# Begin addresses of weight-part and activation buffers moved by multiples of 32 and 16 bytes in a two-layer fp32 encoder

## The chip, the core and the metric

The kernel runs on one core of one Trainium2 chip. The metric is the device time of one execution, in microseconds: 2274.97 us for the kernel before, the median of 3 runs (2274.55 to 2275.17).

## What is computed

An encoder trunk of two layers over 256 tokens of width 2048, in fp32. Layer 0 is neighbourhood attention (16 heads of 128, a learned position bias) and a squared-ReLU MLP of hidden width 8192; layer 1 is a dilated attention of three groups with partial rotary, merged by softmax weights, and a second MLP of the same size:

```python
for i in range(DEPTH):
    hn = rms_norm(x, mixer_norms[i])
    x = x + (neighbourhood_attention if i == 0 else dilated_attention)(hn, ...)
    x = x + jnp.square(jax.nn.relu(rms_norm(x, g) @ w1)) @ w2
return rms_norm(x, final_norm)
```

Nearly all the work is products of a 256-row activation with weight matrices that are read once from memory, some 426 MB of them.

## The kernel before

**Numbers in two parts.** A weight or an activation v in fp32 is split into hi, which is v rounded to the format float32r, and lo, which is v minus hi, rounded in the same way. A product is then hi·hi + hi·lo + lo·hi, three matmuls into the same accumulator (`three`, L193; its lines are L195, L196, L197). ScalarE (ACT) makes hi by a copy (L190), VectorE (DVE) makes lo by a subtraction (L191); both lines are in `split`.

**Steps.** The program is a list of 400 steps. A step holds four 128x512 blocks of weights, loaded by SyncE into a buffer `w` (three of these), and split into parts two blocks at a time: `two_parts` (L138) takes a buffer `wh` and a buffer `wl` of 1024 elements a partition from a pool with four buffers of each. The matmuls of a step come in four quarters; between the quarters stand the splits for the step two ahead, and attention's small work.

**Who streams.** In the query and key products of attention (`gemm_cols`, L200) the weights are the stationary operand and the activation streams: L220 streams hi and lo of the activation side by side (512 columns) past wh, L222 streams hi alone (256 columns) past wl. Everywhere else (`gemm_rows`, `gemm_pair`) a 128x128 piece of the activation is stationary and 512 columns of wh or wl stream past it. Every matmul is preceded by its own weight load (PEld), which lies beside the matmul ahead of it.

**Activations.** They lie in buffers of 2048 elements a partition: four of `xT` (the normalized input of a layer, transposed) and four of the tag `o`, which serve as `oT` (attention's output), `hT` (the MLP's hidden values) and, at times, as score and bias buffers.

**The x-steps.** In the MLP some pairs of blocks are multiplied by a scheme that takes seven products where eight would be needed. For these the step forms sums of weight blocks (`sums`, with the parts `hs` and `ls`), and sums of activation blocks (`xs` in the first product of an MLP; in the second a smaller tile that is also named `hs`). These parts lie in the stage's own pool, outside the pools that the change touches. Seven products of three matmuls take the forms (xs with hs), (xs with wh), (xT with hs) and (xT with wh), so the same matmul form appears with operands from different pools.

**Order.** The order of instructions on each engine is written out by hand; no scheduler decides it.

**Where the buffers begin.** In the program as built, the pools are laid one behind the other in each partition. `xT`'s four buffers begin at the bytes 33952, 42144, 50336, 58528; the four of `o` at 66720 and on by 8192; `w`'s three at 99488 and on by 8192; `wh`'s at 124064 and on by 4096; `wl`'s at 140448 and on by 4096. All of these leave the remainder 32 when divided by 128. The tiles of a stage's own pool (`xs`, `sums`, `hs`, `ls`, `C`, the attention tiles) begin at 159616 and behind; all that enter float32r matmuls leave the remainder 0, as does the identity matrix `ident`.

Of the kernel before, what the change touches and what calls it, by code (L numbers as in the profile page):

```python
# [9 lines left out]
F32R = mybir.dt.float32r  # L10
# [4 lines left out]
P = 128  # L15
T = 256
# [31 lines left out]
def tile_encoder(ctx: ExitStack, tc: tile.TileContext, ins, out):  # L48
# [3 lines left out]
    xpool = ctx.enter_context(tc.tile_pool(name="xpool", bufs=4))  # L52
    opool = ctx.enter_context(tc.tile_pool(name="opool", bufs=4))
    wpool = ctx.enter_context(tc.tile_pool(name="wpool", bufs=3))
    hlpool = ctx.enter_context(tc.tile_pool(name="hlpool", bufs=4))
# [15 lines left out]
    class Part:  # L71

        pool = guard = None
# [15 lines left out]
    def scratch(shape, name):  # L89

        if part.name[0] == "f":
            return part.pool.tile(shape, F32, name=name, tag="t", bufs=2)
        return part.pool.tile(shape, F32, name=name, tag="p", bufs=5)
# [41 lines left out]
    def add(engine, out, a, b):  # L135
        engine.tensor_tensor(out=out, in0=a, in1=b, op=ALU.add)  # L136

    def two_parts(s, u):  # L138
        hi = hlpool.tile([P, 2, 512], F32R, name="wh", tag="wh")
        lo = hlpool.tile([P, 2, 512], F32R, name="wl", tag="wl")  # L140
        for a in range(2):
            s.hi[2 * u + a], s.lo[2 * u + a] = hi[:, a, :], lo[:, a, :]
        return hi, lo
# [45 lines left out]
    def split(dst_hi, dst_lo, src):  # L189
        nc.scalar.copy(dst_hi, src)  # L190
        nc.vector.tensor_tensor(out=dst_lo, in0=src, in1=dst_hi.bitcast(F32), op=ALU.subtract)  # L191
# [159 lines left out]
    def last_sum(q, tb, c, out):  # L351

        C, own = q["C"][:, 2 * tb + c, :], q[STD[tb, c]]
        if (tb, c) == (1, 0):
            subtract(nc.vector, out, own, C)
        else:
            add(nc.vector, out, C, own)


    class Norm:  # L360
# [18 lines left out]

        def parts(self, c, half):  # L380
            if half == 0:
                self.xT[c] = xpool.tile([P, 4, 2, T], F32R, name="xT", tag="xT")
            xT = self.xT[c]
            if 2 * c + half in self.pairs:
                raw = scratch([P, 2, T], "gx")
                for a in range(2):
                    k = 4 * c + 2 * half + a
                    nc.scalar.activation(raw[:, a, :], self.tp[:, a, :], AF.Copy, scale=gT[:, self.n, k:k + 1])
                self.sums[2 * c + half] = part.pool.tile([P, 2, 3, P], F32R, name="xs", tag="xs", bufs=len(self.pairs))
                sums_and_parts(raw, xT, half, self.sums[2 * c + half])  # L390
                return
            for which, a in [(which, 2 * half + a) for which in ("hi", "lo") for a in range(2)]:
                src = self.tp[:, a % 2, :]
                hi, lo = xT[:, a, 0, :], xT[:, a, 1, :]
                if self.perm:
                    src = src.rearrange("p (j s r) -> p r s j", s=4, r=4)
                    hi = hi.rearrange("p (r s j) -> p r s j", s=4, r=4)
                    lo = lo.rearrange("p (r s j) -> p r s j", s=4, r=4)
                g = gT[:, self.n, 4 * c + a:4 * c + a + 1]
                if which == "hi":  # L400
                    nc.scalar.activation(hi, src, AF.Copy, scale=g)
                elif self.perm:
                    gx = scratch([P, T], "gx")
                    nc.vector.tensor_scalar(out=gx.rearrange("p (r s j) -> p r s j", s=4, r=4), in0=src,
                                            scalar1=g, scalar2=None, op0=ALU.mult)
                    nc.vector.tensor_tensor(out=xT[:, a, 1, :], in0=gx, in1=xT[:, a, 0, :].bitcast(F32),
                                            op=ALU.subtract)
                else:
                    nc.vector.scalar_tensor_tensor(out=lo, in0=src, scalar=g, in1=hi.bitcast(F32),
                                                   op0=ALU.mult, op1=ALU.subtract)  # L410
# [31 lines left out]
    def sums_and_parts(raw, t, half, sums):  # L442

        c = scratch([P, 3, P], "c")
        a11, a21, a12, a22 = raw[:, 0, :P], raw[:, 0, P:], raw[:, 1, :P], raw[:, 1, P:]
        subtract(nc.vector, c[:, 0, :], a11, a21)
        subtract(nc.vector, a21, a21, a22)
        subtract(nc.vector, c[:, 1, :], a11, a21)
        subtract(nc.vector, c[:, 2, :], a12, c[:, 1, :])
        hi, lo = (t[:, 2 * half:2 * half + 2, h, :] for h in range(2))  # L450
        nc.scalar.copy(hi, raw)
        nc.scalar.copy(sums[:, 0], c)
        subtract(nc.vector, lo, raw, hi.bitcast(F32))
        subtract(nc.vector, sums[:, 1], c, sums[:, 0].bitcast(F32))
# [36 lines left out]
    def at(i, pe=None, post=None, quarter=1):  # L491
        later.append((i, pe, post, quarter))
# [3 lines left out]
    def at_after(i, n, f):  # L496
        later_after.append((i, n, f))
# [20 lines left out]
    na_oT = [None] * 4  # L518
# [12 lines left out]
    class NaHeads:  # L531
# [73 lines left out]

        def s3_post(self, h):
            if na_oT[self.c] is None:
                na_oT[self.c] = opool.tile([P, 4, 2, T], F32R, name="oT", tag="o")
            t = na_oT[self.c]
            split(t[:, h, 0, :], t[:, h, 1, :], self.o[:, 0, :])  # L610

# [16 lines left out]
    for c in range(4):  # L628
# [5 lines left out]
        i = steps.index(made[0])  # L634
# [5 lines left out]
        i = steps.index(made[0])  # L640
# [26 lines left out]
    def ffn(norm, w1, w2, next_norm, next_done):  # L667
        for g in range(4):
            last = g == 3
            pairs2 = (3, 5) if last else (2, 3, 5)  # L670
            hT, sums = [None] * 4, {}

            def hidden(made, q, cp, hT=hT, sums=sums, pairs2=pairs2, last=last):
                i = steps.index(made[-1]) + 1

                def squared_relu(tb, n):
                    c = q["C"][:, 2 * tb + n, :]
                    nc.scalar.activation(c, c, AF.Relu, scale=norm.r[:, tb:tb + 1])  # L678
                    nc.scalar.activation(c, c, AF.Square)

                for m, (tb, n) in enumerate(QUARTERS):
                    made[-1].after[m].append(lambda tb=tb, n=n: last_sum(q, tb, n, q["C"][:, 2 * tb + n, :]))
                    at_after(i, m, lambda tb=tb, n=n: squared_relu(tb, n))
                for r in range(4):
                    held = {}

                    def pe(r=r, held=held):
                        held["t"] = t = ps.misc()
                        for a in range(2):
                            f = 2 * r + a  # L690
                            for tb in range(2):
                                nc.tensor.transpose(t[:, a, tb * P:(tb + 1) * P],  # L692
                                                    q["C"][:, 2 * tb + f // 4, f % 4 * P:(f % 4 + 1) * P], ident)

                    def post(r=r, held=held):
                        c, half, pair = 2 * cp + r // 2, r % 2, 4 * cp + r
                        if half == 0:
                            hT[c] = opool.tile([P, 4, 2, T], F32R, name="hT", tag="o")
                        if pair in pairs2:
                            raw = part.pool.tile([P, 2, T], F32, name="h", tag="h", bufs=2)  # L700
                            nc.scalar.copy(raw, held["t"])

                            def parts_of(c=c, half=half, raw=raw, pair=pair):
                                sums[pair] = part.pool.tile([P, 2, 3, P], F32R, name="hs", tag="hsum", bufs=3)
                                sums_and_parts(raw, hT[c], half, sums[pair])
                            steps[i + (3 if cp else 2 * r - 1)].after[1].append(parts_of)
                        else:
                            to = hT[c][:, 2 * half:2 * half + 2]
                            split(to[:, :, 0, :], to[:, :, 1, :], held["t"])

                    at(i + 1, pe, post, quarter=r)
# [66 lines left out]
    dil_oT = [None] * 2  # L778
# [21 lines left out]
    class DilHeads:  # L800
# [91 lines left out]

        def s3_post(self, h):
            if dil_oT[self.hh] is None:
                dil_oT[self.hh] = opool.tile([P, 4, 2, T], F32R, name="oT", tag="o")
            t = dil_oT[self.hh]
            src = self.o[:, 0, :].rearrange("p (r s j) -> p j s r", r=4, s=4)
            hi = t[:, h, 0, :].rearrange("p (j s r) -> p j s r", r=4, s=4)
            lo = t[:, h, 1, :].rearrange("p (j s r) -> p j s r", r=4, s=4)
            nc.scalar.copy(hi, src)  # L900
            nc.vector.tensor_tensor(out=lo, in0=src, in1=hi.bitcast(F32), op=ALU.subtract)
# [132 lines left out]
    for i, s in enumerate(steps):  # L1034
# [31 lines left out]
        if i:  # L1066
            p = steps[i - 1]
# [67 lines left out]
```

## Time and profile before

| what | value |
|---|---|
| median of 3 runs | 2274.97 us |
| profiled execution, from its first to its last instruction | 2273.7 us |
| its mean granted TensorE clock | 0.999 |
| matmuls, busy | 2252.3 us, 10,904 of them |
| DVE busy | 1876.6 us |
| ACT busy | 1263.4 us |
| read from memory | 426.38 MB |

The profiled execution lies 1.3 us below the median of the runs. In the profile "PE" is the matmul and "PEld" the weight load. A matmul's duration reaches from its start to the modelled end of its last column, so that it overlaps the next one: the pace is read from the starts in the timeline, and the duration tells how one matmul differs from another of the same form. A view by tile gives the least, the median and the greatest duration of every form that reads or writes a tile.

### The profile page before, as it was taken

Reading aid. Unit: us, or ns where it says so; the run is one execution under the profiler, and the core shown is the slowest. Engines: PE = TensorE matmul, PEld = TensorE weight load, DVE = VectorE, ACT = ScalarE, POOL = GpSimd, SP = SyncE. Lnnn points to the kernel's source line nnn. Section 1 sums busy time; section 2 is a strip of 40 time slices with the busy share of each in tenths; the row PEclk is TensorE's granted clock in tenths of the full one; section 3 lists DMA queues with packets and bytes.
Section 4 is the critical chain, followed back from the end, with each engine's and each line's share of the span. In section 5 each row is a group of like instructions: output and inputs, shape, how many; then the busy total and the mean of one; then the engine's idle time right before and its main releaser. Section 6 shows DMA issues by size and latency. Waiting matters only on the chain.

```text
span 2273.7 us, 28396 instructions
## 1 busy us (share of the span) xinstructions
PE 2252.3 (99%) x10904; PEld 1882.5 (83%) x10904; DVE 1876.6 (83%) x2215; ACT 1263.4 (56%) x1570; POOL 0.7 (0%) x6
## 2 busy tenths in 40 slices
PE   9999999999999999999999999999999999999998
PEld 7888888888888888888888888888888888888886
DVE  6777666899999999989877667757999999999988
ACT  6545445665565565565444544456665665665664
POOL 0000000000000000000000000000000000000000
PEclk9999999999999999999999999999999999999999
DMA  7556655556656666655555545454666666666664
GB/s 252 185 178 187 185 181 167 185 185 208 199 185 205 203 185 195 205 179 190 206 177 183 178 167 185 167 173 149 209 199 196 190 198 193 198 195 196 202 213 138
DMA packets 110728, 430.33 MB, mean 189 GB/s; under 512 B 23872, under 2 KB 24448, under 8 KB 92160
## 3 DMA queue, kind: packets, MB, share of 16 engines
q1 hardware_dynamic: 109920, 426.82, 58.5%
q8 instruction: 85, 1.39, 0.2%
q10 hardware_dynamic: 672, 1.70, 0.2%
q14 instruction: 51, 0.42, 0.1%
HBM read 426.38 MB, written 2.10 MB: 188 GB/s over the span
## 4 chain that ended last, share of the span: by engine, by line
PE 92%; DVE 4%; ACT 2%; issue 1%; DMA 0%; SPq 0%; ACTq 0%; DVEq 0%
PE banks L195 23%; PE banks L197 23%; PE banks L196 23%; PE banks L220 13%; PE banks L222 7%; DVE wl L191 1%; PE banks L692 1%; DVE C L136 1%; DVE sums L136 1%; ACT wh L190 0%; PE banks L378 0%; ACT hs L176 0%; ACT C L678 0%; DVE C L133 0%; PE banks L890 0%
## 5 line engine op out<-in xcount | busy, mean ns | idle before, releaser
L191 DVE TENSOR_TENSOR wl<-w,wh 128x1024 fp32r<-128x1024 f32 (+1 forms) x802 | 966.0, 1218 | 297.0 <-ACT wh L190 293.3
L190 ACT CAST wh<-w 128x1024 fp32r<-128x1024 f32 (+1 forms) x802 | 829.6, 1048 | 589.3 <-PE banks L197 324.1
L220 PE MATMUL banks<-xT,wh 128*128 128x512 f32 x1280 | 453.6, 398 | 0.0
L195 PE MATMUL banks<-wh,xT 128*128 128x512 f32 x1104 | 435.0, 394 | 0.0
L197 PE MATMUL banks<-wh,xT 128*128 128x512 f32 x1104 | 430.8, 390 | 0.0
L196 PE MATMUL banks<-wl,xT 128*128 128x512 f32 x1104 | 429.8, 389 | 0.0
L222 PE MATMUL banks<-xT,wl 128*128 128x256 f32 x1280 | 358.0, 280 | 0.0
L195 PE MATMUL banks<-wh,hT 128*128 128x512 f32 x804 | 316.6, 394 | 1.9 <-DVE hT L191 1.9
L197 PE MATMUL banks<-wh,hT 128*128 128x512 f32 x804 | 313.6, 390 | 0.0
L196 PE MATMUL banks<-wl,hT 128*128 128x512 f32 x804 | 312.9, 389 | 0.0
L220 PEld LDWEIGHTS banks<-xT,wh 128*128 128x128 f32 x1280 | 241.0, 188 | 53.6
L197 PEld LDWEIGHTS banks<-wh,xT 128*128 128x128 f32 x1104 | 207.2, 188 | 43.9
L222 PEld LDWEIGHTS banks<-xT,wl 128*128 128x128 f32 x1280 | 242.0, 189 | 0.5 <-DVE wl L191 0.2
L196 PEld LDWEIGHTS banks<-wl,xT 128*128 128x128 f32 x1104 | 207.5, 188 | 41.3
L195 PEld LDWEIGHTS banks<-wh,xT 128*128 128x128 f32 x1104 | 207.5, 188 | 41.3
L176 ACT CAST hs<-sums 128x1536 fp32r<-128x1536 f32 x92 | 136.6, 1485 | 177.6 <-DVE sums L136 177.6
L195 PEld LDWEIGHTS banks<-wh,hT 128*128 128x128 f32 x804 | 151.0, 188 | 33.9 <-DVE hT L191 3.3
L197 PEld LDWEIGHTS banks<-wh,hT 128*128 128x128 f32 x804 | 150.9, 188 | 32.0
L196 PEld LDWEIGHTS banks<-wl,hT 128*128 128x128 f32 x804 | 151.1, 188 | 30.7
L133 DVE TENSOR_TENSOR ls<-sums,hs 128x1536 fp32r<-128x1536 f32 x92 | 161.1, 1751 | 0.3 <-ACT hs L176 0.3
L136 DVE TENSOR_TENSOR sums<-w 128x1024 f32<-128x1024 f32 x92 | 112.0, 1218 | 0.0
L195 PE MATMUL banks<-wh,oT 128*128 128x512 f32 x192 | 76.4, 398 | 0.0
(188 smaller groups left out, 2295.4 us busy)
## 6 DMA issues: line engine op xcount, KB each, us to landing
w<-in_ffn_w_dram SPq DMA_DIRECT2D x512, 512.0 KB, 4.9
w<-in_dil_wqkv_dram SPq DMA_DIRECT2D x72, 1024.0 KB, 4.9
w<-in_na_wqkv_dram SPq DMA_DIRECT2D x47, 1024.0 KB, 5.1
w<-in_na_wo_dram SPq DMA_DIRECT2D x16, 1024.0 KB, 4.8
w<-in_dil_wo_dram SPq DMA_DIRECT2D x8, 1024.0 KB, 4.9
bias<-in_rpb_dram SPq DMA_DIRECT2D x32, 96.0 KB, 9.7
out_dram<-x SPq DMA_DIRECT2D x8, 256.0 KB, 2.5
x<-in_x_dram SPq DMA_DIRECT2D x3, 512.0 KB, 9.3
```

The costliest lines, as they stand in the source:

```text
L133: engine.tensor_tensor(out=out, in0=a, in1=b, op=ALU.subtract)
L136: engine.tensor_tensor(out=out, in0=a, in1=b, op=ALU.add)
L176: nc.scalar.copy(s.hs, s.sums)
L190: nc.scalar.copy(dst_hi, src)
L191: nc.vector.tensor_tensor(out=dst_lo, in0=src, in1=dst_hi.bitcast(F32), op=ALU.subtract)
L195: nc.tensor.matmul(o, left[0], right[0], start=start, stop=False)
L196: nc.tensor.matmul(o, left[0], right[1], start=False, stop=False)
L197: nc.tensor.matmul(o, left[1], right[0], start=False, stop=stop)
L220: nc.tensor.matmul(o, s.hi[a][:, cs], xt.rearrange("p h t -> p (h t)"), start=first, stop=False)
L222: nc.tensor.matmul(o[:, :T], s.lo[a][:, cs], xt[:, 0, :], start=False, stop=last)
L692: nc.tensor.transpose(t[:, a, tb * P:(tb + 1) * P], q["C"][:, 2 * tb + f // 4, f % 4 * P:(f % 4 + 1) * P], ident)
```

## The change

A helper `staggered` allocates the buffers `wh`, `wl`, `xT`, `oT` and `hT`. It asks the pool for a buffer that is longer by four steps, and uses the part of it that begins 0, 1, 2 or 3 steps behind the buffer's start, by turns for each tag. The step is 8 elements (32 bytes) for the weight parts and 4 elements (16 bytes) for the activations. Nothing else is changed.

```diff
+    turn_of = {}
+
+    def staggered(pool, shape, name, tag, step):
+
+        i = turn_of[tag] = (turn_of.get(tag, -1) + 1) % 4
+        n = 1
+        for d in shape[1:]:
+            n *= d
+        t = pool.tile([P, n + 4 * step], F32R, name=name, tag=tag)[:, i * step:i * step + n]
+        if len(shape) == 3:
+            return t.rearrange("p (a n) -> p a n", n=shape[2])
+        return t.rearrange("p (a h n) -> p a h n", h=shape[2], n=shape[3])
+
     def two_parts(s, u):
-        hi = hlpool.tile([P, 2, 512], F32R, name="wh", tag="wh")
-        lo = hlpool.tile([P, 2, 512], F32R, name="wl", tag="wl")
+        hi = staggered(hlpool, [P, 2, 512], "wh", "wh", 8)
+        lo = staggered(hlpool, [P, 2, 512], "wl", "wl", 8)
...
-                self.xT[c] = xpool.tile([P, 4, 2, T], F32R, name="xT", tag="xT")
+                self.xT[c] = staggered(xpool, [P, 4, 2, T], "xT", "xT", 4)
...
-                na_oT[self.c] = opool.tile([P, 4, 2, T], F32R, name="oT", tag="o")
+                na_oT[self.c] = staggered(opool, [P, 4, 2, T], "oT", "o", 4)
...
-                            hT[c] = opool.tile([P, 4, 2, T], F32R, name="hT", tag="o")
+                            hT[c] = staggered(opool, [P, 4, 2, T], "hT", "o", 4)
...
-                dil_oT[self.hh] = opool.tile([P, 4, 2, T], F32R, name="oT", tag="o")
+                dil_oT[self.hh] = staggered(opool, [P, 4, 2, T], "oT", "o", 4)
```

On all five engines the built program has the same instructions in the same order with the same waits as before; only line numbers differ (by 13 behind the helper) and addresses. The longer buffers move the pools behind them as well. In the program as built, the places at which operands begin now leave these remainders when divided by 128:

| buffers | before | changed |
|---|---|---|
| wh, wl (a pair always has the same turn) | 32, 32, 32, 32 | 32, 64, 96, 0 |
| xT | 32, 32, 32, 32 | 32, 112, 64, 16 |
| w | 32 | 32 |
| the stage's own tiles that enter float32r matmuls | 0 | 0 |

The four xT buffers get remainders that differ by more than 16, since each buffer also begins 64 bytes later than a multiple of 128 behind the one ahead. The buffers of the tag `o` have the same set, but the turn there passes over the score and bias tiles, which take a buffer without a turn.

## The prediction

> **What bounds the kernel now.** I read the page's shares and its chain first, for the engine that sets the end.
>
> ```profile
> span 2273.7 us, 28396 instructions
> PE 2252.3 (99%) x10904; PEld 1882.5 (83%) x10904; DVE 1876.6 (83%) x2215; ACT 1263.4 (56%) x1570; POOL 0.7 (0%) x6
> PEclk9999999999999999999999999999999999999999
> PE 92%; DVE 4%; ACT 2%; issue 1%; DMA 0%; SPq 0%; ACTq 0%; DVEq 0%
> ```
>
> Matmuls fill 99% of the span, the chain that ended last is 92% matmul, and the granted clock is full throughout. PE is without work for 2273.7 − 2252.3 = 21.4 us. So the time is the number of matmuls times their pace, and a change that moves no instruction can act in two ways alone: through the pace of matmuls, or through an engine that becomes slow enough to hold PE up.
>
> The pace is in the timeline of PE. Two pieces: the end of a first MLP product, and the end of an x-step.
>
> ```profile
> 485.06 0.39 PE L196 MATMUL banks<-wl,xT 128*128 128x512 f32 x1
> ...
> 487.33 0.39 PE L197 MATMUL banks<-wh,xT 128*128 128x512 f32 x1
> ```
>
> ```profile
> 417.23 0.40 PE L196 MATMUL banks<-ls,xT 128*128 128x512 f32 x1
> 417.47 0.40 PE L197 MATMUL banks<-hs,xT 128*128 128x512 f32 x1
> 417.70 0.40 PE L195 MATMUL banks<-wh,xT 128*128 128x512 f32 x1
> 417.93 0.39 PE L196 MATMUL banks<-wl,xT 128*128 128x512 f32 x1
> ```
>
> In the first, ten starts take 2.27 us: 227 ns a matmul. In the second the form is the same (a stationary piece of xT, 512 columns stream), but the starts are 240 and 230 ns apart, in steps of 10 ns: about 235. The duration says the same in finer steps: 0.39 against 0.40. The view by tile has it for all matmuls of a kind (columns: count, then least, median and greatest duration in ns). First what streams wl, then what streams the x-steps' own parts:
>
> ```profile
> L196 PE MATMUL banks<-wl,xT x1104: 387/389/398, 57.5 to 2176.2; 128*128 128x512 f32 x184
> L196 PE MATMUL banks<-wl,hT x804: 387/389/398, 487.8 to 2262.7; 128*128 128x512 f32 x161
> L196 PE MATMUL banks<-wl,oT x192: 387/389/395, 303.8 to 1573.2; 128*128 128x512 f32 x192
> L196 PE MATMUL banks<-wl,xs x48: 397/397/397, 416.5 to 2170.0; 128*128 128x512 f32 x48
> L196 PE MATMUL banks<-wl,hs x44: 396/397/397, 504.8 to 2245.7; 128*128 128x512 f32 x44
> ```
>
> ```profile
> L195 PE MATMUL banks<-hs,xT x48: 397/397/397, 417.0 to 2170.5; 128*128 128x512 f32 x48
> L196 PE MATMUL banks<-ls,xT x48: 397/397/397, 417.2 to 2170.7; 128*128 128x512 f32 x48
> L197 PE MATMUL banks<-hs,xT x48: 395/395/395, 417.5 to 2171.0; 128*128 128x512 f32 x48
> ```
>
> ```profile
> L195 PE MATMUL banks<-hs,xs x96: 389/395/505, 414.1 to 2168.4; 128*128 128x512 f32 x96
> L196 PE MATMUL banks<-ls,xs x96: 387/393/398, 414.4 to 2168.6; 128*128 128x512 f32 x96
> L197 PE MATMUL banks<-hs,xs x96: 389/397/400, 414.7 to 2168.9; 128*128 128x512 f32 x96
> ```
>
> This is the finding on which the forecast rests. Of the 2100 matmuls in the first three rows the median is 389; where one operand comes from the stage's pool, all of them take 395 to 397, with no spread; where both do, the medians are 393 to 397. Shape, type and neighbours are the same. What differs is the remainder at which the operand begins: 32 (mod 128) in the pools that the change touches, 0 in the stage's pool. No spread means that it isn't a collision with what DVE or ACT happen to do at that moment. So before the change nearly all the work stands in the one fast case, (32, 32), and the slow cases known are (0, 32), (32, 0) and, a little less, (0, 0).
>
> **The change part by part.** No instruction is added, removed or moved. The edit to wh and wl, and those to xT, oT and hT, have one effect: 32 and 32 become pairs of (32, 64, 96, 0) with (32, 112, 64, 16). I count by the remainder to 64, since 0 and 32 are all that the trace tells apart. Over the built program, among the matmuls that stream wh or wl while the next piece of xT, oT or hT is loaded, the shares are: both 32, 15%; both 0, 12%; one 0 and one 32, 27%; the activation at 16 or 48, 47%. The matmuls concerned are 3 × (1104 + 804 + 192) = 6300 (lines L195 to L197).
>
> - Both 32: 389 as now, 0 us.
> - Both 0: the rows hs,xs average (395 + 393 + 397) / 3 = 395, so +6 ns: 0.12 × 6300 × 6 = 4.5 us.
> - One of each: rows of 397, 397, 397, 395, the last products of a kind being lower, so +7: 0.27 × 6300 × 7 = 11.9 us.
> - 16 or 48: the trace has no such operand. From below, 0 (it could act as 32 does; nothing below 387 occurs in any row of this form, so a gain is excluded to within 2 ns). From above, +8, the worst steady median less 389. I take +5, between, nearer the upper end, because two operands that differ are the slow case in every row there is: 0.47 × 6300 × 5 = 14.8 us, with ends 0 and 23.7.
>
> Together 31 us. Then the query and key products, 1280 pairs of L220 and L222:
>
> ```profile
> 1149.79 0.39 PE L220 MATMUL banks<-xT,wh 128*128 128x512 f32 x1
> ...
> 1153.95 0.39 PE L220 MATMUL banks<-xT,wh 128*128 128x512 f32 x1
> ```
>
> ```profile
> 1225.94 0.40 PE L220 MATMUL banks<-xT,wh 128*128 128x512 f32 x1
> ...
> 1229.12 0.40 PE L220 MATMUL banks<-xT,wh 128*128 128x512 f32 x1
> ```
>
> Twelve pairs take 4.16 us in the first stretch, 347 ns each; nine take 3.18 us in the second, 353 each. All operands are at 32 in both, so here a second, slower rhythm of +6 exists without any difference in address, and holds for many pairs. That cuts two ways: the fast rhythm can be lost by a small push, and addresses aren't the only cause. The kernel has both rhythms now, with a mean somewhere between. I take +4 for the seven eighths of pairs that get unequal remainders: 1280 × 7/8 × 4 = 4.5 us, with ends −2 (all in the fast rhythm) and +8 ns: −2.2 to +9 us.
>
> The x-steps keep (xs, hs); their mixed products change places among slow cases (a part becomes both 0, one ns less): under 1 us, left out.
>
> DVE and ACT read and write the moved buffers. Rows for tiles at 32 and at 0:
>
> ```profile
> L191 DVE TENSOR_TENSOR wl<-w,wh 128x1024 fp32r<-128x1024 f32 x798 | 963.4, 1220 | 297.0 <-ACT wh L190 293.3
> L136 DVE TENSOR_TENSOR sums<-w 128x1024 f32<-128x1024 f32 x92 | 112.0, 1218 | 0.0
> ```
>
> All at 32 takes 1220, output at 0 and inputs at 32 takes 1218: nothing. What covers this zero is DVE's 297 us of idle time ahead of its splits; a slowdown of a tenth in them (96 us) would still fit into it as a whole, though less well in the MLP, where DVE is densest. DMA queues: the buffer w stays at 32, and loads go where they went. With PE slower, the splits are a little earlier against it, and some of PE's 21.4 idle us go: −2 us.
>
> Sum: 31 + 4.5 − 2 = 33.5 us on the profiled 2273.7, or 2274.97 + 33.5 = about 2308 for a run.
>
> **A rule against it.** The row first: 397 with no spread against 389, for one form of matmul, by operands' places. The Trainium skill, in "SBUF — State Buffer", section "Who interferes with whom", says that TensorE and ScalarE never wait for anyone in reading this memory, and that TensorE has one port for what streams and another for weight loads. By that the change costs nothing, and the sum is 0. The page doesn't speak of where in a partition an operand begins, and the rows show a dependence on something like it; but that two pools differ is shown, not that the remainder is what differs.
>
> **Rivals.**
>
> *No effect* (20%). The slow rows could come from the stage's pool lying at other addresses altogether (above 159616), or from the break in rhythm at each switch between pools: hs,xs runs only six matmuls long, the mixed ones three. For it: the second rhythm in the query products with no change of address. Against it: 2100 matmuls cross many switches between buffers at 32 with a median of 389, and all 48 of a mixed kind have the same 397. Price 0: 2275 us, within 0.2% (4.5 us), which is about what a measurement of this kernel can tell from no change.
>
> *Faster* (12%). The mechanism: equal remainders are themselves a collision, which the turn removes. Its place would be the fixed part of a matmul: 512 columns take 227 and the next 256 take 347 − 227 = 120, so a column costs 107 / 256 = 0.418 ns and 13 ns of each matmul are fixed. If even a tenth of that went, 10,904 × 1.3 = 14 us would be saved: 2261; a half, 71 us: 2204. It decides from the first matmul. Against it: (0, 0) and (32, 32) differ, though both are equal; and unequal ones are the slowest. A small gain is open without it, the slow rhythm of the query products lost: 2 us.
>
> *Much slower* (13%). A pair that differs by 16 or 48 could cost two such slips of 7 or 8 ns, where one of 0 with 32 costs one; it decides as soon as an activation lies at 16 or 48. 47% of 6300 at 15 ns is 44 us in place of 14.8, and the query pairs at +16: 2275 + 16 + 44 + 18 − 2 = 2351.
>
> *The change does not do what it says*: the offsets might cancel against the longer buffers. They don't for wh and wl (a buffer grows by 128 bytes); for activations they give other remainders than 0, 16, 32 and 48 on from 32, which the sum already has.
>
> **How the numbers follow.** Main case 55%, 2285 to 2328 by its ends (31 us with 0 or 8 for the unknown, −2 or +9 from the query products), point 2308. No effect 20%, faster 12%, much slower 13%. Slower by over 0.2%: 55 + 13 = 68%; within 0.2%: 20%; faster: 12%. The range must hold 8 of 10: the whole main case with its neighbourhood, no effect, and the smallest gains: 2269 to 2332; left out are most of the faster case and of the much slower one.
>
> **What would show it.** If the main case holds, the row of wl with xT has a median of some 394 in place of 389, with several fixed values side by side (389, 395, 397) instead of one; the same row for hs with xs doesn't move; DVE's 1220 stays. PE's busy time grows by as much as the span, and its idle time doesn't. If the 389 stays, addresses' remainders aren't the cause and the time is 2275. If the median drops below 387, the faster case is right. If DVE's or ACT's durations move, the sum has left out its largest part.

## The result, and the profile after

The changed kernel takes 2295.79 us (median of 4 runs, 2295.58 to 2297.14), the kernel before beside it 2274.9: a ratio of 1.0093, with a 95% interval of 1.0081 to 1.0105. It is slower by 20.9 us. The page of the changed kernel (line numbers are larger by 13):

```profile
span 2294.1 us, 28396 instructions
PE 2274.9 (99%) x10904; PEld 1885.4 (82%) x10904; DVE 1876.7 (82%) x2215; ACT 1263.0 (55%) x1570; POOL 0.7 (0%) x6
PE 91%; DVE 5%; ACT 2%; issue 1%; DMA 0%; SPq 0%; ACTq 0%; DVEq 0%
L204 DVE TENSOR_TENSOR wl<-w,wh 128x1024 fp32r<-128x1024 f32 (+1 forms) x802 | 966.2, 1218 | 317.9 <-ACT wh L203 313.7
```

The span grew by 20.4 us and PE's busy time by 22.6; DVE and ACT have the busy time that they had, with the same mean for a split (1218 ns on both pages, where the row holds one form more than the prediction's row of 1220), and DVE stands idle ahead of its splits for 21 us longer. Nothing waits more; matmuls are slower. The view by tile of the changed kernel shows which (count, then least, median and greatest duration in ns):

```profile
L209 PE MATMUL banks<-wl,xT x1104: 387/394/404, 57.1 to 2195.5; 128*128 128x512 f32 x184
L209 PE MATMUL banks<-wl,hT x804: 387/394/404, 490.4 to 2283.5; 128*128 128x512 f32 x161
L209 PE MATMUL banks<-wl,oT x192: 387/394/404, 304.0 to 1586.5; 128*128 128x512 f32 x192
L209 PE MATMUL banks<-wl,xs x48: 388/397/398, 418.4 to 2189.2; 128*128 128x512 f32 x48
L208 PE MATMUL banks<-hs,xT x48: 388/394/399, 418.8 to 2189.7; 128*128 128x512 f32 x48
L210 PE MATMUL banks<-hs,xs x96: 388/392/397, 416.5 to 2188.0; 128*128 128x512 f32 x96
```

The median of the three large kinds went from 389 to 394, and the two forms shown that had one fixed value (wl with xs, hs with xT: 397, 397, 397) now spread from 388 to 399. The least, 387, is where it was. The last row, hs with xs, has moved too: L197 had 389/397/400 before, and its own tiles keep their remainders.

All starts of the trace, from each matmul to the next, add up as follows (us; "main" is wh or wl streaming past xT, oT or hT, "query and key" is L220 with L222):

| part | before | changed | difference |
|---|---|---|---|
| main, steps under 260 ns | 6170 x 227.44 ns = 1403.3 | 6184 x 231.85 ns = 1433.8 | +30.5 |
| main, the longer steps (waits, transposes) | 43.6 | 38.1 | −5.5 |
| query and key products | 452.5 | 452.5 | 0.0 |
| x-steps' products with own parts | 258.0 | 255.3 | −2.7 |
| all else | 101.2 | 99.7 | −1.5 |
| sum | 2258.6 | 2279.4 | +20.8 |

### The profile page after: what moved, and what is told of

The parts are those of the page before. It is cut to its first block, busy times and chain, and to the rows that moved or that the text cites. A ratio compares the mean times of both kernels' runs of the same rounds, so it can differ in the third digit from the quotient of the medians.

```text
span 2294.1 us, 28396 instructions
## 1 busy us (share of the span) xinstructions
PE 2274.9 (99%) x10904; PEld 1885.4 (82%) x10904; DVE 1876.7 (82%) x2215; ACT 1263.0 (55%) x1570; POOL 0.7 (0%) x6
## 4 chain that ended last, share of the span: by engine, by line
PE 91%; DVE 5%; ACT 2%; issue 1%; DMA 0%; SPq 0%; ACTq 0%; DVEq 0%
PE banks L208 23%; PE banks L209 23%; PE banks L210 23%; PE banks L233 13%; PE banks L235 6%; DVE wl L204 2%; PE banks L705 1%; DVE C L136 1%; DVE sums L136 1%; DVE C L133 0%; ACT wh L203 0%; PE banks L391 0%; ACT hs L189 0%; ACT C L691 0%; PE banks L903 0%
## 5 line engine op out<-in xcount | busy, mean ns | idle before, releaser
L204 DVE TENSOR_TENSOR wl<-w,wh 128x1024 fp32r<-128x1024 f32 (+1 forms) x802 | 966.2, 1218 | 317.9 <-ACT wh L203 313.7
L209 PE MATMUL banks<-wl,xT 128*128 128x512 f32 x1104 | 434.8, 394 | 0.0
L208 PE MATMUL banks<-wh,hT 128*128 128x512 f32 x804 | 320.3, 398 | 1.4 <-DVE hT L204 1.4
L210 PE MATMUL banks<-wh,hT 128*128 128x512 f32 x804 | 316.9, 394 | 0.0
L136 DVE TENSOR_TENSOR sums<-w 128x1024 f32<-128x1024 f32 x92 | 112.0, 1218 | 0.0
```

Of the source, the lines that this page charges most:

```text
L208: nc.tensor.matmul(o, left[0], right[0], start=start, stop=False)
L209: nc.tensor.matmul(o, left[0], right[1], start=False, stop=False)
L210: nc.tensor.matmul(o, left[1], right[0], start=False, stop=stop)
```

## The experiments

Two theories stood at the start. The *pair theory* is the prediction's: each pair of remainders has its own pace. The *switch theory* is its rival: an operand that changes its place breaks the rhythm, and any constant place would find it again. In brackets behind a time stand its ratio to the kernel before, run beside it, and the 95% interval of that ratio. The kernels below use the change's helper with a table of offsets in elements, one for each turn, and, unless it is said otherwise, buffers that are 128 bytes longer:

```diff
-        t = pool.tile([P, n + 4 * step], F32R, name=name, tag=tag)[:, i * step:i * step + n]
+        at = places[tag][i]
+        t = pool.tile([P, n + 32], F32R, name=name, tag=tag)[:, at:at + n]
```

### Constant places, no turns: all at 0, and weights at 64 with activations at 32

```diff
+    places = {"wh": (24, 24, 24, 24), "wl": (24, 24, 24, 24), "xT": (24, 24, 24, 24), "o": (24, 24, 24, 24)}
```

> All float32r operands of the moved buffers begin at the remainder 0 (mod 128), constantly, as the stage's own tiles do already; no turns. Pair theory (the forecast's: each pair of remainders has its own pace, 32 with 32 fast, 0 with 0 at +5 to +6 ns): 6300 x 5.5 ns = +35 us, about 2310 us, median of wl with xT 393 to 395. Switch theory (a pace is lost when the place of an operand changes, and a constant place finds the fast rhythm whatever it is): no change of place is left, not even in the x-steps, so 389 and 2266 to 2275 us.

```diff
+    places = {"wh": (8, 8, 8, 8), "wl": (8, 8, 8, 8), "xT": (0, 0, 0, 0), "o": (0, 0, 0, 0)}
```

> wh and wl constantly at 64 (that is 0 mod 64), the activations constantly at 32: unequal, but no turns. Pair theory: 6300 x 7 ns = +44 us and some +5 from the query products, about 2320 us, the median of wl with xT at 396 or 397. Switch theory: as before the change, 2272 to 2278 us, median 389.

All at 0 took 2290.78 us (1.0069, 1.0054 to 1.0084); weights at 64 took 2307.14 (1.014, 1.0123 to 1.0157). The view by tile of the second:

```profile
L211 PE MATMUL banks<-wl,xT x1104: 389/394/400, 57.8 to 2206.0; 128*128 128x512 f32 x184
L211 PE MATMUL banks<-wl,hT x804: 389/394/400, 493.6 to 2294.4; 128*128 128x512 f32 x161
```

With a constant unequal place the pace is lost without any turn: the least is now 389, what was the median, and the mean of the main steps is 233.17 ns. That speaks against the switch theory, as long as places are counted to 128; counted to 256, the longer buffers still change place here, and the theory is settled only further down. The first run fits neither theory well: +15.5 us, less than half of what equal remainders at 0 were to cost.

### The stage's own tiles moved to 32

```diff
     part = Part()
+    shift = small.tile([P, 8], F32, name="shift", tag="shift", bufs=1)
     part.begin("attention")
```

> The kernel before with one 32-byte tile added ahead of the stage's own pools, so that these too begin at 32 (mod 128); nothing else. Both theories: the x-steps' 1104 matmuls fall from about 232.8 ns to 227, -6 us: 2268 to 2270 us, and hs with xT goes from 397 to 389. If neither place nor change of place is the cause of the x-steps' 397 (a third theory: the region of memory, or the form of the step), it stays 2275.

It took 2273.29 us (0.999, 0.9981 to 1.0). The view by tile of this kernel:

```profile
L196 PE MATMUL banks<-hs,xT x48: 389/389/389, 417.6 to 2168.5; 128*128 128x512 f32 x48
L197 PE MATMUL banks<-wl,xs x48: 389/389/395, 417.1 to 2168.0; 128*128 128x512 f32 x48
L221 PE MATMUL banks<-xT,wh x1280: 387/398/775, 7.9 to 1450.4; 128*128 128x512 f32 x183
```

The 397 of the x-steps has become 389, again with no spread, by 32 bytes of address and nothing else. So the prediction's reading that these rows come from the place of an operand holds, and neither the region of memory nor the form of the step is their cause. Which property of the place it is, this run can't tell: it makes the remainders equal and sets the distance between the operands to a multiple of 256 bytes at once. The rows of hs with xs fell as well, from medians of 395 and 397 to 389, though their two remainders were equal before (0 and 0) and are equal now (32 and 32). By the starts the x-steps give 6.2 us (258.0 to 251.8). But the query and key products, whose own operands haven't moved, take 455.9 for 452.5: the median of their long matmul is 398 for 395. They took back over half.

### Half of the change

```diff
+    places = {"wh": (0, 0, 0, 0), "wl": (0, 0, 0, 0), "xT": (0, 20, 8, 28), "o": (0, 20, 8, 28)}
```

> Activations alone by turns, at the remainders 32, 112, 64, 16 that the change gives them; weight parts stay at 32. Pair theory: a quarter of 6300 at 0 ns, a quarter (32 with 64) at +7, half (32 with 112 or 16) at +5: +27 us, 2302 us. Switch theory: the place changes once in 24 to 48 matmuls in place of once in 12, so less than half of the change's +21 us: 2278 to 2286 us.

```diff
+    places = {"wh": (0, 8, 16, 24), "wl": (0, 8, 16, 24), "xT": (0, 0, 0, 0), "o": (0, 0, 0, 0)}
```

> Weight parts alone by turns (32, 64, 96, 0), activations constantly at 32. Pair theory by the remainder to 64 with the paces measured since (32 with 32 227.4 ns, 64 with 32 233.2): half of 6300 at +5.8 = +18 us, and +1 from the query products: 2292 to 2296 us. If each change of place costs as well, more than that: 2298 to 2304 us. If the two parts of the change added, this run and that of the activations alone (+21.4 us) would have to give the whole change's +20.9, so 0 here: 2275 us.

The activations' half alone took 2296.67 us (1.0095, 1.008 to 1.011), the weights' half alone 2300.82 (1.0111, 1.0098 to 1.0125). Each half costs as much as the whole or more. Neither is strictly a half: both kernels make all the moved buffers 128 bytes longer (in the change the activations' are longer by 64), and what that costs without any offset is measured below. Both miss what the pair theory gave: 2302 for the activations, 2292 to 2296 for the weights. The weights' run lies where each change of place was to cost something as well; but weights at a constant 64 are slower still, so that turns aren't needed for it.

### Is 32 special?

```diff
+    places = {"wh": (16, 16, 16, 16), "wl": (16, 16, 16, 16), "xT": (16, 16, 16, 16), "o": (16, 16, 16, 16)}
```

> All moved buffers constantly at 96, own tiles at 0. If the pace goes by the remainder to 64 (as the forecast counted), this is the kernel before: 2273 to 2278 us, median of wl with xT 389. If 32 of 128 alone is the fast place, it is like the run with all at 0: 2288 to 2312 us.

```diff
+    places = {"wh": (4, 4, 4, 4), "wl": (4, 4, 4, 4), "xT": (4, 4, 4, 4), "o": (4, 4, 4, 4)}
```

> All moved buffers constantly at 48, own tiles at 0. If what counts is that the two remainders are equal, it lies between the kernel before and the run with all at 0: 2275 to 2291 us. If 32 is the one fast place, 2295 to 2310 us.

All at 96 took 2291.67 us (1.0072, 1.0058 to 1.0086), all at 48 took 2297.92 (1.0098, 1.0084 to 1.0112). All at 96 has equal remainders, and 32 to 64, and is as slow as all at 0. That ends the count by 64. But these kernels share a thing that I had overlooked in the change as well: with buffers 128 bytes longer, neighbours lie 4224 and 8320 bytes apart, no longer 4096 and 8192. Grouped by the distance of the two operands' places, the next stationary piece less what streams, to 256, the main steps of the run with all at 0 fall in two:

| kernel | distance 0 (mod 256) | distance 128 |
|---|---|---|
| before | 5961 x 227.3 ns | none |
| all at 0 | 3058 x 228.1 | 2903 x 232.5 |
| all at 96 | 3058 x 228.2 | 2903 x 232.5 |
| all at 48 | 3058 x 231.4 | 2903 x 232.9 |

(Steps under 260 ns between two of 512 columns; the places are those of the program as built.) In the kernel before, every pair of wh, wl with xT, oT, hT lies at distance 0, as all buffers were multiples of 2048 bytes apart. Hence a third theory, the *distance theory*: the fast rhythm needs a distance of 0 (mod 256). All at 48 says that this isn't enough: there both distances are slow. So do the products of hs with xs in the kernel before, which lie at distance 0 and have medians of 393 to 397; they come six at a time, each six behind a step whose distance isn't 0. The run with the weights alone by turns fits: 782 of its 5961 steps, 13%, are at distance 0 (228.2 ns).

### The distance by itself

Longer buffers with no offset at all:

```diff
+    places = {"wh": (0, 0, 0, 0), "wl": (0, 0, 0, 0), "xT": (0, 0, 0, 0), "o": (0, 0, 0, 0)}
```

> The moved buffers are 128 bytes longer and begin at 32 (mod 128) as before: no turns, no offset, only the distance from buffer to buffer grows (4224 and 8320 bytes for 4096 and 8192). Distance theory (new): what counts is the difference of the two operands' places to 256, and longer buffers leave half of the pairs 128 apart: like the runs with all at 0 and all at 96, 2288 to 2293 us. Pair theory with 32 (mod 128) as the one fast place: 2275 us.

And buffers 256 bytes longer, all at 0, which restores the distance at another place:

```diff
+    places = {"wh": (24, 24, 24, 24), "wl": (24, 24, 24, 24), "xT": (24, 24, 24, 24), "o": (24, 24, 24, 24)}
-        t = pool.tile([P, n + 32], F32R, name=name, tag=tag)[:, at:at + n]
+        t = pool.tile([P, n + 64], F32R, name=name, tag=tag)[:, at:at + n]
```

> The moved buffers are 256 bytes longer and all begin at 0 (mod 256), so that any two of them differ by 0 (mod 256), at another place than before. Distance theory: back to the kernel before, 2274 to 2281 us, the median of wl with hT at 389 again. Pair theory with 32 as the one fast place: as the run with all at 0, 2288 to 2293 us.

Longer by 128, no offset: 2292.49 us (1.0075, 1.006 to 1.009). Longer by 256, all at 0: 2280.74 (1.0023, 1.0014 to 1.0032). The distance theory had said 2288 to 2293 and 2274 to 2281. The timeline of PE in the first of these, in one step of the output product of attention; between the first two rows the pairs lie 128 apart, between the last three 0:

```profile
305.02 0.40 PE L212 MATMUL banks<-wh,oT 128*128 128x512 f32 x1
...
307.13 0.39 PE L212 MATMUL banks<-wh,oT 128*128 128x512 f32 x1
...
308.06 0.40 PE L210 MATMUL banks<-wh,oT 128*128 128x512 f32 x1
...
309.46 0.39 PE L210 MATMUL banks<-wh,oT 128*128 128x512 f32 x1
...
310.59 0.40 PE L212 MATMUL banks<-wh,oT 128*128 128x512 f32 x1
```

At distance 128, nine steps take 2.11 us, 234 ns each. At distance 0, the first six behind other matmuls still take 1.40 us, 233 ns each, and the five behind them 1.13, 226 each. So the fast rhythm has to be found again, and that is what is left of the switch theory. All main steps of this trace, counted from the last change of distance or the last other matmul, give (mean ns):

| steps | distance 0 | distance 128 |
|---|---|---|
| 1 to 3 | 868 x 230.7 | 853 x 232.1 |
| 4 to 6 | 736 x 228.2 | 627 x 232.5 |
| 7 to 12 | 970 x 227.2 | 857 x 233.2 |
| 13 to 24 | 452 x 226.7 | 506 x 232.7 |

At distance 0 the pace settles within some ten steps; at 128 it never does, however long the place stays. A change of place by itself therefore costs a few ns in a few steps, and the distance costs 6 ns in every step. The six matmuls of hs with xs may be too few to settle; that fits these rows, but no run tests it by itself.

The view by tile of the second kernel has the old medians again:

```profile
L211 PE MATMUL banks<-wl,xT x1104: 387/389/398, 57.8 to 2181.5; 128*128 128x512 f32 x184
L211 PE MATMUL banks<-wl,hT x804: 387/389/402, 489.1 to 2268.1; 128*128 128x512 f32 x161
```

It stays 5.5 us above the kernel before: 2.8 of it in the main products (1449.7 us with the longer steps, for 1446.9) and 3.4 in the query and key products (455.9). Half of its main steps lie 0 apart to 512 and half 256, and they have 227.7 and 227.8 ns, so the distance counts to 256 and not to 512. The place itself seems to have a small effect too; for the query and key products that isn't shown, since they took the same 455.9 in the run above in which their own operands hadn't moved.

### The turns without longer distances

```diff
+    places = {"wh": (0, 8, 16, 24), "wl": (0, 8, 16, 24), "xT": (0, 4, 8, 12), "o": (0, 4, 8, 12)}
-        t = pool.tile([P, n + 32], F32R, name=name, tag=tag)[:, at:at + n]
+        t = pool.tile([P, n + 64], F32R, name=name, tag=tag)[:, at:at + n]
```

> The change's turns without its shift of distance: offsets 0, 32, 64, 96 for weight parts and 0, 16, 32, 48 for activations, but each buffer longer by 256 bytes, so that only the offsets make the places differ. Distance theory with the mean paces per distance (mod 256) found in the changed kernel and the runs since (0: 228.5, -16: 228.9, 16: 231.1, 32: 232.7, 48: 232.9, -32: 233.0, -48: 232.1, -64: 229.9, -80: 230.2, -96: 233.6 ns), over the 16 pairs of turns: a mean of 231.0 ns, +3.6 x 6184 = 22 us, less some 5 of waits: 2290 to 2297 us, so that offsets and longer buffers each cost nearly the whole +20.9 alone. If the longer buffers were what the change costs and the offsets are harmless: 2275 to 2281 us.

It took 2297.68 us (1.0099, 1.0082 to 1.0116), 22.1 above the kernel before, at the upper edge of what the distance theory gave, slightly over it. So the offsets cost the whole loss by themselves, buffers longer by 128 bytes cost 17.3 by themselves, and the change, which has both, 20.9. They don't add; by the distance theory a pair that isn't at distance 0 can't lose it twice. The change's own lengths, 128 bytes more for weight parts and 64 for activations, were not run without its offsets.

### Two faster versions

The own tiles of the MLP alone at 32, attention's left at 0:

```diff
             self.pool = self.guard.__enter__()
+            if name[0] == "f":
+                self.shift = self.pool.tile([P, 8], F32, name="shift", tag="shift")
```

> The kernel before with a 32-byte tile ahead of the own pool of the MLP stages alone, so that the x-steps' parts begin at 32 and attention's tiles stay at 0. Pair theory, after the run with all own tiles at 32 (x-steps 258.0 to 251.8 us, query and key products 452.5 to 455.9): the x-steps' gain of 6 us without the loss in the query products: 2268 to 2271 us. If the query products' slower rhythm in that run was chance, or if PE's waits take the gain back, 2272 to 2275 us.

And with it the weight parts of the query and key products 32 bytes below the activation (mod 256):

```diff
-        hi = hlpool.tile([P, 2, 512], F32R, name="wh", tag="wh")
-        lo = hlpool.tile([P, 2, 512], F32R, name="wl", tag="wl")
+        at = 56 if s.cols else 0
+        hi, lo = (hlpool.tile([P, 1024 + 64], F32R, name=n, tag=n)[:, at:at + 1024].rearrange("p (a n) -> p a n", n=512)
+                  for n in ("wh", "wl"))
...
+            s.cols = True
```

> The MLP's own tiles at 32 as in the fastest run so far, and the weight parts of the query and key products 32 bytes below the activation (mod 256), all others at a distance of 0. In the run with activations by turns, pairs of L220 and L222 at that distance took 347.0 ns and nearly never the slow rhythm, against 349.0 at equal places: 1280 x 2 ns = -2.5 us on 2268.75, 2265 to 2268 us. If that pace was chance, 2268 to 2271 us.

The first took 2268.75 us (0.9971, 0.996 to 0.9982), the second 2265.97 (0.9959, 0.9946 to 0.9971). Both are faster than the kernel before and than the changed one. The page and the view by tile of the second:

```profile
span 2263.7 us, 28396 instructions
PE 2241.0 (99%) x10904; PEld 1884.5 (83%) x10904; DVE 1876.3 (83%) x2215; ACT 1263.3 (56%) x1570; POOL 0.7 (0%) x6
```

```profile
L199 PE MATMUL banks<-hs,xT x48: 389/389/389, 414.8 to 2161.1; 128*128 128x512 f32 x48
L200 PE MATMUL banks<-wl,xs x48: 389/389/389, 414.3 to 2160.6; 128*128 128x512 f32 x48
L224 PE MATMUL banks<-xT,wh x1280: 389/390/775, 7.6 to 1443.1; 128*128 128x512 f32 x183
L226 PE MATMUL banks<-xT,wl x1280: 277/282/415, 8.1 to 1443.4; 128*128 128x256 f32 x183
```

The x-steps keep their 389, and the long matmul of the query products has a median of 390 for 395: a pair takes 346.9 ns by the starts, and 2% of pairs take 351 ns or more, for 349.0 and 15% in the version without it. Where 512 and 256 columns alternate, a distance of −32 is better than 0; where 512 follow 512, it costs 6 ns. I had no ground for that beyond the pairs in the run with activations by turns.

## Why the prediction was right, and where it wasn't

The direction and its bound were right: PE's pace alone moved, DVE's mean for a split stayed, PE's busy time grew by as much as the span, and the median of wl with xT is 394, as forecast. 2295.79 lies in 2269 to 2332, 12 us under the point. One sign failed: the rows of hs with xs were not to move, and L197's median went from 397 to 392.

*The x-steps' rows as the evidence.* Right in that 397 with no spread came from 32 bytes of address, as moving those tiles showed. Too neat in that all mixed rows were said to have 395 to 397 (L197 of wh with xs, not shown there, has 393 throughout), and in that hs with xs were taken for the price of remainders 0 and 0: in the run with all at 0, the steps at distance 0 took 228.1 ns, less than 1 ns over the kernel before.

*The count by the remainder to 64, with both 32 at 0 ns.* Wrong; this is the step that failed. What the runs show in its place is the distance of the two operands to 256, and the buffers' greater length, which the prediction only checked for whether it cancels the offsets, changes that distance by itself. By the starts in the changed kernel the classes as I had cut them have these means, against 227.4 before:

| class (mod 64) | forecast | measured |
|---|---|---|
| both 32 | +0 | 872 x 230.7 ns: +3.3 |
| both 0 | +6 | 702 x 231.6: +4.2 |
| one 0, one 32 | +7 | 1587 x 233.1: +5.7 |
| activation at 16 or 48 | +5 | 2800 x 231.6: +4.2 |

The classes hardly differ, and the fast one isn't fast. That the sum comes out near is luck, since too little for one class met too much for the three others: 31 us forecast for the pace, and 6170 x (231.85 − 227.44) = 27.2 us measured. Cut by distance the same steps do differ: 451 at 0 with 229.9 ns, 439 at −16 with 228.4, 414 at −64 with 230.0, 328 at 128 with 232.5, 329 at 96 with 234.1. Even so the distance accounts for only about a quarter of the variance of these steps.

*The query and key products, +4.5 us.* Mis-sized: 0.0 measured. Their rhythms exchanged places: with the streaming activation at 64 and the weights at 32 a pair takes 347.0, at 32 and 64 351.0.

*Waits, −2 us, and x-steps under 1 us.* The waits were right: the main products grew by 25.0 us with their waits, so that the waits gave back 2.2 there. Mis-sized were the terms put at nothing: all else gave back 1.5 and the x-steps 2.7. With 31 − 27.2 and the query products these make the 12.7 us by which the sum of 33.5 lies above the 20.8 of the trace. The ends of the main case, 2285 and 2328, don't follow from its terms either, which give 2287 and 2322; the result lies within both.

*The rivals.* No effect fell with the result. The faster case's mechanism, that equal places collide, is contradicted: distance 0 has the fastest settled pace where 512 columns follow 512. Much slower didn't come: with the activation at 16 or 48 a step took 231.6 ns, +4.2 and not two slips, and no distance took more than 234.1. The Trainium skill's rule in "SBUF — State Buffer", section "Who interferes with whom", that TensorE never waits on anyone, can't be read as a statement on pace: longer buffers alone, without an offset, cost 17.3 us. Whether TensorE waits for anything in that time, no run shows. The prediction's remark that the page doesn't speak of where an operand begins goes too far: the page says which beginnings are allowed, and gives no time for them.

What stays open is why. That the stream and the weight load beside it get in each other's way, in a pattern that repeats after 256 bytes, would fit; it is argued and not shown. Nor is it settled why 48 is slow at distance 0, why −16 and −64 are better than −32, or how the stage's own tiles in attention push the query products into the slower rhythm.

## What to carry to other kernels

Where a kernel is bound by matmuls that each load their own weights, the begin addresses of both operands are worth a look: here 512 columns found the fast rhythm and kept it when the two lay a multiple of 256 bytes apart (all at 48 was the exception), and padding or offsetting buffers broke it, at 4 to 6 ns of 227 for most matmuls that it reached. Rows of one form with two fixed durations are the sign; moving the slower operand by 32 bytes was worth 6.8 us. A change of a buffer's length is a change of address of everything behind it, and two such changes need not add.

## What was unexpected in the hardware

- A pool's pitch acts on its own: 128 bytes more between buffers, with no offset and no other change, cost 0.75% (2292.49 for 2275.22 us).
- Matmuls settle in rhythms that hold for many steps. At distance 0 the settled step is 226 to 227 ns; at 128 it mostly alternates between 229 or 230 and 237 or 238, up to 24 steps after the last change of place.
- The best distance depends on the lengths that alternate: 0 for 512 after 512, −32 for 512 with 256 (346.9 ns a pair for 349.0).
